# The first MLP's up projection: all 11 column groups as block products of operands without the norm's row factor

## The chip, the cores and the metric

The kernel runs on one core of one Trainium2 chip, as one launch. The metric is the device time of one execution in microseconds. The core's engines are TensorE (PE in the profile, with PEld for its weight loads), VectorE (DVE), ScalarE (ACT), GpSimd (POOL) and SyncE (SP); each works through its own instructions in order and waits on semaphores that the others, or transfers, raise.

## The reference

A trunk of four residual layers over 512 tokens (S) of 1024 features (D), all in float32: attention, MLP, short convolution, MLP. Cut to what matters here:

```python
def conv_ffn(h, norm_g, w_up, conv_w, w_down):
    xn = rms_norm(h, norm_g)                    # h * rsqrt(mean(h*h) + EPS) * norm_g
    u = causal_dwconv(xn @ w_up, conv_w)        # w_up: 1024 x 5632, three taps along the tokens
    g, val = u[..., :D_FF], u[..., D_FF:]       # D_FF = 2816
    return (jax.nn.silu(g) * val) @ w_down      # w_down: 2816 x 1024

h = h + attention_mixer(...);   h = h + conv_ffn(...)   # the MLP of this change
h = h + short_conv_mixer(...);  h = h + conv_ffn(...)
```

The norm multiplies h by two factors: a gain for each feature, and a factor for each token (row), `rsqrt(mean(h*h) + EPS)`. Since the up projection sums over features, the row factor may stand before it or behind it.

## The kernel before

**Precision.** Every float32 operand is split into a high half (ScalarE, `whi`, `p_hi`) and a low half (VectorE, `wlo`, `p_lo`: the operand minus its high half), and each product of blocks is three matmuls: high by high, high by low, low by high.

**Seven products.** Activations lie as features by tokens. A group of an up projection is two column blocks (128 columns each) of the gate and two of the value. Seen as a 2 x 2 block matrix (features 0 to 511 and 512 to 1023; tokens 0 to 255, LEFT, and 256 to 511, RIGHT), its result is made from seven products instead of eight, with sums of blocks ahead of them and sums of results behind them: p1, p7, p3, p6, p2, q5, q4. Each is 24 matmuls of 256 columns (L1078): two column blocks, four blocks of 128 features, three terms. Class `Sevens` plans a group in seven slots (`slot(g, s)`): a slot issues one product, and around it the loads, splits and sums of this group, the group before and the next. The activations' forms of a product (`forms`: p1 is one block, p7 a difference, p6 a sum, and so on) are made once for all groups. The weights' sums that do not depend on the activations are tables in DRAM, "7", "6" and, for the first MLP, "4" (tiles `t`): `table_steps` makes them by DMAs that Pool issues, a plain copy and then an accumulating one, in pairs that build on each other (L114 the accumulating ones, L117 the plain ones).

**The first MLP** has 11 groups. The first two (`PLAIN = 2, 0`) are not made of seven products but of eight plain blocks: `up_seven` runs 192 matmuls of 512 columns (L336 to L338) on `hs_a` and `hs_b`, the halves of h times gain times row factor. While they run, `prepare` makes X_prep, px_prep and Y_prep, again with the row factor, and the forms of the seven products from them; `normed` and `gate_one` do the gates of the plain groups. The norm (class `Norm`) sums squares on ScalarE and VectorE feature block by feature block as the residual adds (L853) of the attention's output projection finish. 12 small matmuls bring the sums together (L410) and spread the row factor over the partitions (L396). The second MLP already works as the change does: all groups are products of h times gain, by `RawForms`, and the results are multiplied by the row factor afterwards (`scaled`).

**The down projection** (`mlp`, second half) makes products of its own in seven phases p1, p7, p2, p6, p3, q5, q4, each over six blocks of the 22 feature blocks (`GROUPS`). Its weights' sums, too, are partly made by accumulating DMAs that Pool issues onto loaded tiles (L289: `p_hi_chain`, `q_lo_chain` and others); ScalarE and VectorE then split them (L315, L316). VectorE joins the results to h (L1609).

**Order.** Most instructions get their place on their engine from a scheduler, which weighs the work by costs. Those in `pin` (`tc.keep_in_program_order`) keep the order of the program among each other; all of Pool's DMAs of the tables and of the weights' sums are pinned. With `strict[0]` on, all of ScalarE's and VectorE's work is pinned too. `norm.finish(at, rows)` puts the small matmuls off by so many microseconds of planned TensorE time.

**Tables.** `FAR` and `BETWEEN` say how many steps of the second MLP's tables are issued after the first MLP's and after its down projection; the others are issued in the short convolution.

Of the kernel before, what the change touches and what calls it, by code (L numbers as in the profile page):

```python
# [57 lines left out]
def trunk(  # L58
# [40 lines left out]
    def table_steps(layer):  # L99

        w = ffn_w_up[layer]
        for n in "76" if layer else "764":
            for g, m in CHUNKS[layer]:
# [3 lines left out]
        for g, m in CHUNKS[layer]:  # L107
            for rows in (slice(0, 256), slice(256, 512)):
                for step in range(4 if layer else 6):
                    n = "764"[step // 2]  # L110
                    to = tables[layer, n, g][rows, 0:m * 256]
                    if step % 2:
                        src = block(*((0, 1), (0, 0), (1, 0))[step // 2], g, m)
                        pin(nc.gpsimd.dma_start(to, src[rows, :], accum_op=ALU.add))  # L114
                    else:
                        src = block(1, 1, g, m) if step == 0 else tables[layer, "76"[step // 2 - 1], g][:, 0:m * 256]
                        pin(nc.gpsimd.dma_start(to, src[rows, :]))  # L117
                    yield

    def table_of(layer, n, group):  # L120
        g, m = next(c for c in CHUNKS[layer] if c[0] <= group < c[0] + c[1])
        return tables[layer, n, g][:, (group - g) * 256:(group - g + 1) * 256].rearrange("(k p) c -> p k c", p=P)

    work_scope = ExitStack()
# [355 lines left out]
    def want_ffn(layer, pairs=NF):  # L480
        for j in range(pairs):
            want(ffn_w_up[layer], 0, 8, j * P, P)
            want(ffn_w_up[layer], 0, 8, DFF + j * P, P)

# [10 lines left out]

    want_ffn(0, 2 * PLAIN[0])

# [8 lines left out]
    def mixed(g):  # L506
        return (ap_.tile([P, 4, S], F32R, tag="o_hi", name=f"o_hi{g}", bufs=2),
                ap_.tile([P, 4, S], F32R, tag=("o_lo", "dl")[g], name=f"o_lo{g}"))
# [445 lines left out]
    dl = ap_.tile([P, 4, S], F32R, tag="dl", name="dl")  # L954
# [13 lines left out]
    sums_far = table_steps(0)  # L968
    next(sums_far)
    fill(PRE)  # L970
    for g in range(len(units) + 2):
        for _ in range(2):
            next(sums_far, None)
# [16 lines left out]

    run(sums_far)
    sums_far = table_steps(1)

    def sum_far(n):
        for _ in range(n):
            next(sums_far, None)

    sum_far(FAR)

    def residual_out(o, acc, nxt):  # L1000
        dve.tensor_tensor(h[:, o, :], acc, h[:, o, :], op=ALU.add)
        nxt.feed(o, h[:, o, :])

    norm = Norm("n1", 0)
    run(output_part((4,), range(2), "c"))
    run(output_part(range(4), (3,), "b"))
    fetch(AHEAD - 1)
    for o in range(4):
        residual(o, last[o])
        norm.halves(o, h[:, o, :])  # L1010
    run(output_part((5,), range(2), "c"))
    run(output_part((6, 7), range(2), "a"))
    fetch(AHEAD)
    for o in range(4, ND):
        run(output_part((o,), (2, 3), "a"))
        residual(o, last[o])
        norm.halves(o, h[:, o, :])
    for o in range(ND):
        norm.squares(o, h[:, o, :])
    norm.finish(LATE)  # L1020
    attn.close()


# [16 lines left out]
    class Blocks:  # L1040
# [3 lines left out]
        def __init__(self, place, layer):  # L1044
            self.layer, self.place, self.parts = layer, place, {}

        def at(self, j, n):
            start = 0 if j < HEAD else HEAD if j < HF else HF
            if start not in self.parts:
                pool_, n_, tag = {0: (self.place, 8, "head"), HEAD: (hsp, HF - HEAD, "hs_b"), HF: (hsp, HF, "hs_a")}[start]  # L1050
# [32 lines left out]
    class Sevens:  # L1083

        def __init__(self, name, mp, groups, block_of):
            self.name, self.mp, self.groups, self.block_of = name, mp, groups, block_of
            self.forms = {n: [mp.tile([P, 4, HT], F32R, tag=f"{n}_{i}", name=f"{n}_{i}{name}") for i in ("hi", "lo")] for n in FORMS}
            self.st, self.wides, self.table, self.fours, self.scaled = {}, {}, None, False, False
# [705 lines left out]
```

## Time and profile before

| | |
|---|---|
| median of 3 runs | 1122.13 us (1121.94 to 1123.9) |
| the profiled execution | 1121.57 us, its span 1119.8 us, clock 1.00 |
| TensorE busy | 1109.3 us, 99% of the span, 7803 matmuls |
| VectorE busy | 958.8 us, 86% |
| ScalarE busy | 680.4 us, 61% |
| Pool busy | 174.3 us, 16% |
| moved by DMA | 220.90 MB |

Times in the rows of the profile are from the start of the span; the prediction is made against the profiled execution and then put to the median. The first MLP's up projection runs from 273.91 us, its down projection to 610.77 us. A row of a group of instructions reads: line, engine, operation, what it writes and reads, how many; then busy microseconds and mean nanoseconds of one, and the idle time of the engine ahead of them with what ended it. A row of the timeline reads: start, duration, engine, line, operation, and in brackets how long the engine had been idle and what released it.

### The profile page before, as it was taken

To read this page: it belongs to the slowest core of one execution; us is meant where nothing else is said; L and a number is where in the kernel's file an instruction comes from. 1 tells how busy PE (TensorE), PEld (TensorE's weight loads), DVE (VectorE), ACT (ScalarE), POOL (GpSimd) and SP (SyncE) were. 2 spreads that over 40 slices of the span, in tenths; PEclk is the share of its full clock that TensorE was granted. 3 is DMA by queue.
4 is the path that set the end of the run, shared out by engine and by line. 5 is a ranking of instruction groups with operands and counts; after the bars stand their busy time and mean duration, and the time that the engine had idled before them with its cause. 6 is when DMAs were issued, how large, how long until landed. Compare 5 with 4: busy or idle time off the path is not lost.

```text
span 1119.8 us, 19731 instructions
## 1 busy us (share of the span) xinstructions
PE 1109.3 (99%) x7803; PEld 1011.9 (90%) x7803; DVE 958.8 (86%) x1482; ACT 680.4 (61%) x1006; POOL 174.3 (16%) x203
## 2 busy tenths in 40 slices
PE   9999999999999999999999999999999999999998
PEld 7888787878899999999999889988999999998886
DVE  6798988987899787888979899767899999999886
ACT  7466676655466667676547355445666656667553
POOL 4011111111111110014401101110112221014300
PEclk9999999999999999999999999999999999999999
DMA  6668777677888787699997955697879877899951
GB/s 195 178 175 199 177 186 196 164 197 196 245 206 199 189 212 192 195 297 198 224 260 195 238 143 141 130 275 178 207 179 218 204 189 189 217 262 205 230 154 57
DMA packets 180012, 220.90 MB, mean 197 GB/s; under 512 B 7788, under 2 KB 143516, under 8 KB 179920
## 3 DMA queue, kind: packets, MB, share of 16 engines
q0 software_dynamic: 48384, 97.43, 43.9%
q1 hardware_dynamic: 131376, 122.14, 34.7%
q8 instruction: 61, 1.00, 0.4%
q14 instruction: 31, 0.25, 0.1%
q10 hardware_dynamic: 160, 0.07, 0.0%
HBM read 214.64 MB, written 53.48 MB: 239 GB/s over the span
## 4 chain that ended last, share of the span: by engine, by line
PE 82%; DVE 7%; DMA 5%; issue 3%; ACT 2%; SPq 0%; ACTq 0%; DVEq 0%; POOLq 0%
PE psb L1078 28%; PE psa L1078 11%; PE psb L1673 10%; PE psa L1673 7%; PE psb L336 4%; PE psb L338 4%; PE psb L337 4%; PE psb L710 2%; PE psa L807 2%; DVE wlo L316 1%; DMA Xc<-in_conv_w_in 1%; DMA raw<-in_conv_w_in 1%; DMA raw<-in_conv_w_out 1%; PE psc L782 1%; PE psa L338 1%
## 5 line engine op out<-in xcount | busy, mean ns | idle before, releaser
L1078 PE MATMUL psb<-p_lo,whi_p 128*128 128x256 f32 x480 | 135.1, 282 | 0.0
L315 ACT ACTIVATE whi<-raw 128x1024 fp32r<-128x1024 f32 (+2 forms) x81 | 83.3, 1029 | 85.3 <-PE psb L337 27.9
L1078 PE MATMUL psb<-p_hi,wlo_p 128*128 128x256 f32 x480 | 135.0, 282 | 0.0
L1078 PE MATMUL psb<-p_hi,whi_p 128*128 128x256 f32 x480 | 134.8, 281 | 0.0
L316 DVE TENSOR_TENSOR wlo<-raw,whi 128x1024 fp32r<-128x1024 f32 (+2 forms) x81 | 95.8, 1183 | 28.0 <-ACT whi L315 27.6
L1078 PEld LDWEIGHTS psb<-p_hi,whi_p 128*128 128x128 f32 x480 | 90.9, 189 | 0.0
L1078 PE MATMUL psb<-q_hi,whi_q 128*128 128x256 f32 x320 | 89.9, 281 | 0.5 <-ACT whi_q L74 0.5
L1078 PEld LDWEIGHTS psb<-p_lo,whi_p 128*128 128x128 f32 x480 | 90.4, 188 | 0.0
L1078 PEld LDWEIGHTS psb<-p_hi,wlo_p 128*128 128x128 f32 x480 | 90.2, 188 | 0.1
L1078 PE MATMUL psa<-p_hi,wlo_p 128*128 128x256 f32 x320 | 90.1, 282 | 0.0
L1078 PE MATMUL psa<-p_lo,whi_p 128*128 128x256 f32 x320 | 90.1, 281 | 0.0
L1078 PE MATMUL psb<-q_lo,whi_q 128*128 128x256 f32 x320 | 90.0, 281 | 0.0
L1078 PE MATMUL psb<-q_hi,wlo_q 128*128 128x256 f32 x320 | 89.9, 281 | 0.0
L1078 PE MATMUL psa<-p_hi,whi_p 128*128 128x256 f32 x320 | 89.8, 281 | 0.0
L336 PE MATMUL psb<-hs_a,whi 128*128 128x512 f32 x192 | 79.3, 413 | 0.0
L338 PE MATMUL psb<-hs_a,wlo 128*128 128x512 f32 x192 | 76.3, 398 | 0.0
L1673 PE MATMUL psb<-act,whi 128*128 128x256 f32 x352 | 63.1, 282 | 0.5 <-DVE act L1031 0.4
L1078 PEld LDWEIGHTS psb<-q_hi,whi_q 128*128 128x128 f32 x320 | 60.6, 189 | 0.8 <-ACT whi_q L74 0.8
L1078 PEld LDWEIGHTS psa<-p_hi,whi_p 128*128 128x128 f32 x320 | 60.6, 190 | 0.1
L1078 PEld LDWEIGHTS psa<-p_lo,whi_p 128*128 128x128 f32 x320 | 60.2, 188 | 0.1
L1078 PEld LDWEIGHTS psb<-q_lo,whi_q 128*128 128x128 f32 x320 | 60.2, 188 | 0.0
L1078 PEld LDWEIGHTS psa<-p_hi,wlo_p 128*128 128x128 f32 x320 | 60.2, 188 | 0.0
(553 smaller groups left out, 3593.6 us busy)
## 6 DMA issues: line engine op xcount, KB each, us to landing
t<-in_ffn_w_up POOLq DMA_DIRECT2D x30, 768.0 KB, 7.8
raw<-in_attn_w_in SPq DMA_DIRECT2D x24, 512.0 KB, 5.4
t<-in_ffn_w_up POOLq DMA_DIRECT2D x12, 1024.0 KB, 10.9
t<-t POOLq DMA_DIRECT2D x14, 768.0 KB, 4.7
X<-in_ffn_w_up SPq DMA_DIRECT2D x20, 512.0 KB, 5.0
Y<-t SPq DMA_DIRECT2D x20, 512.0 KB, 6.7
three<-t SPq DMA_DIRECT2D x20, 512.0 KB, 4.8
W<-in_ffn_w_up SPq DMA_DIRECT2D x20, 512.0 KB, 4.0
```

Of the source, the lines that this page charges most:

```text
L315: return (act.activation(hi[:, at_], raw[:, at_], AF.Copy), dve.tensor_tensor(lo[:, at_], raw[:, at_], f32(hi[:, at_]), op=ALU.subtract))
L316: dve.tensor_tensor(lo[:, at_], raw[:, at_], f32(hi[:, at_]), op=ALU.subtract))
L336: made = [pe.matmul(acc, w[0], rhs[0], start=first, stop=False), pe.matmul(acc, w[0], rhs[1], start=False, stop=False), pe.matmul(acc, w[1 ...
L337: pe.matmul(acc, w[0], rhs[1], start=False, stop=False),
L338: pe.matmul(acc, w[1], rhs[0], start=False, stop=last)]
L710: pe.matmul(ss[e][:, c:c + wide], ql[rows, b * P:n], kl[rows, 0:wide], start=first and b == bs[0], stop=last and b == bs[-1])
L782: pe.transpose(t[:, k * P:(k + 1) * P], w[:, e, k * P:(k + 1) * P], ident)
L807: pe.matmul(out_, w, t[:, first:first + step * (NB - k - 1) + 1:step, :], start=k == 0 and i == 0, stop=k == NB - 1 and i == 1)
L1078: pe.matmul(to, w[a][:, k, c], x[b][:, k, :], start=fresh and i + k + t == 0, stop=i == 1 and k == 3 and t == 2, skip_group_check=not fresh)
L1673: pe.matmul(to, l, r, start=begin and o + t == 0, stop=end and t == 2 and o == (0 if layer else 1), skip_group_check=not fresh)
```

## The change

All 11 groups of the first MLP become seven products; the plain stage with `up_seven`, `prepare`, `normed` and `gate_one` goes. The operands are h times gain, without the row factor: `RawForms.take` writes x_up block by block after each residual add, `make` builds the forms. The squares of the norm are four 1024-wide steps of ScalarE in slot 3 of group 0, their sums four steps of VectorE in slot 4; the small matmuls come later (`LATE` 21 instead of 7), and everything that needs the row factor is held until it is there. The gates of the groups stand in later slots (`tail`). Table "4" is gone: its operand is made by accumulating onto "three". So the first MLP's tables are 24 steps instead of 36, and both MLPs' tables are one sequence: 31 steps (`FAR`) in the attention, 9 (`BETWEEN`) inside the down projection, behind a small Pool instruction `hold` that reads h; before, 8 steps came after the attention and 9 behind the down projection. From the end of the attention's output projection until slot 6 of group 1, ScalarE and VectorE keep program order (`strict`). Two tiles, "four" and "head", are set aside earlier and hold attention tiles until then.

```diff
-NSUMS, NROWS, LATE = 4.0, 3.0, 7.0
+NSUMS, NROWS, LATE = 4.0, 3.0, 21.0
-PLAIN = 2, 0
-FAR, BETWEEN = 8, 9
-CHUNKS = ((2, 3), (5, 3), (8, 3)), ((0, 3), (3, 4), (7, 4))
+FAR, BETWEEN = 31, 9
+CHUNKS = (0, 3), (3, 4), (7, 4)
...
+    sums_far = both_layers()
+    sum_far(1)
     for g in range(len(units) + 2):
-        for _ in range(2):
-            next(sums_far, None)
+        sum_far(min(2, FAR - 1 - 2 * g) if 2 * g < FAR - 1 else 0)
...
         def to_wide(self, g, n, side, acc):
             if self.scaled:
-                dve.tensor_tensor(to, acc, self.row(side), op=ALU.mult)
+                self.norm.scaled(lambda: dve.tensor_tensor(to, acc, self.row(side), op=ALU.mult))
...
-                    if self.fours:
-                        self.load_one(g, "four", self.table("4", g))
+                    c["four"] = c["three" if self.table else "Y"]
+                    if self.scaled and soon:
+                        self.add_block(g, "four", 1, 0)
...
         def tail(p, s):
+            if layer:
+                plan = {0: [(p, 0)], 1: [(p, 1)], 3: [(p, 2)], 4: [(p, 3)], 5: [(p, 4)]}
+            elif p == 0:
+                plan = {4: [(p, 0)], 5: [(p, 1)], 6: [(p, 2), (p, 3)]}
+            else:
+                plan = {0: [(p - 1, 4)], 3: [(p, 0)], 4: [(p, 1)], 5: [(p, 2)], 6: [(p, 3), (p, 4)] if p == HF - 1 else [(p, 3)]}
...
+                if name == "q4" and g == 1 and not layer:
+                    hold = tiny.tile([P, 1], F32, tag="hold", name="hold", bufs=1)
+                    pool.tensor_tensor(hold, h[:, 7, 0:1], h[:, 7, 0:1], op=ALU.add)
+                    sum_far(BETWEEN)
...
         if after_:
             after_.finish()
-            sum_far(BETWEEN)
...
+        strict[0] = True
+        for o in range(4):
+            residual_in_turn(o)
+        raw.make("p1")
+        up.weights_of(0, "p1", "X")
+        raw.make("p7")
+        run(output_part((5,), range(2), "c"))
+        run(output_part((6, 7), range(2), "a"))
+        for o in range(4, ND):
+            run(output_part((o,), (2, 3), "a"))
+            residual_in_turn(o)
+            if o == 4:
+                up.first_sums(0)
+            elif o == 5:
+                raw.make("p6", slice(0, 2))
+        raw.make("p6", slice(2, 4))
+        norm.finish(LATE, LATER)
+        squared = [wides[n] for n in ("ug", "uv", "yg", "yv")]
...
+        norm = mlp(0, mp, blocks, slots_of(up, {
+            (0, 0): lambda: up.weights_of(0, "p6", "three"), (0, 1): lambda: (up.weights_of(0, "p2", "W"), raw.make("p2")),
+            (0, 2): lambda: raw.make("q5"), (0, 3): lambda: (raw.make("q4"), square()), (0, 4): add_squares, (0, 6): lambda: raw.make("p3"),
+            (1, 6): lambda: strict.__setitem__(0, False)}))
```

**Pool's queue in the down projection, before.** `q_hi_chain` and `q_lo_chain` are the weights of phase q4, in the order of its blocks 2 to 5; `t` are tables of the second MLP; `Yc` belongs to the short convolution.

```order
L289 DMA q_hi_chain_0_6196<-in_ffn_w_down 128x2x512
L289 DMA q_lo_chain_0_6230<-in_ffn_w_down 128x512
L289 DMA q_hi_chain_0_6265<-in_ffn_w_down 128x2x512
L289 DMA q_lo_chain_0_6300<-in_ffn_w_down 128x2x512
L117 DMA t_3276<-in_ffn_w_up 256x1024
L114 DMA t_3276<-in_ffn_w_up 256x1024
L117 DMA t_3279<-t_3276 256x1024
L114 DMA t_3279<-in_ffn_w_up 256x1024
```

All four accumulations for q4 stand ahead of the tables; four more steps like these and a ninth follow, then `Yc`. The same place of the changed kernel, where the lines of the two kinds of table steps are L113 and L116:

```order
L289 DMA q_hi_chain_0_6279<-in_ffn_w_down 128x2x512
L289 DMA q_lo_chain_0_6318<-in_ffn_w_down 128x512
L1604 TENSOR_TENSOR hold<-h 128x1
L113 DMA t_1908<-in_ffn_w_up 256x768
L116 DMA t_1906<-in_ffn_w_up 256x1024
L113 DMA t_1906<-in_ffn_w_up 256x1024
L116 DMA t_1909<-t_1906 256x1024
L113 DMA t_1909<-in_ffn_w_up 256x1024
...
L289 DMA q_hi_chain_0_6353<-in_ffn_w_down 128x2x512
L289 DMA q_lo_chain_0_6388<-in_ffn_w_down 128x2x512
```

The accumulations for q4's blocks 4 and 5 have moved from ahead of the tables to behind them (where rows are left out, four more steps like the four above them), and `hold` is new.

**ScalarE at the start of the up projection, before**: splits of the last output weights (`whi<-raw`), halves of the normed h (`hs_a`), squares (`sq_n`):

```order
L372 ACTIVATE hs_a_119<-h,gains 128x512 x3
L381 ACTIVATE sq_n_3391<-h 128x512
...
L315 ACTIVATE whi_3348<-raw_3350 128x1024
L381 ACTIVATE sq_n_3397<-h 128x512
L372 ACTIVATE hs_a_119<-h,gains 128x512 x2
L381 ACTIVATE sq_n_3400<-h 128x512
L315 ACTIVATE whi_3434<-raw_3436 128x1024
```

and in the changed kernel, from the fifth to the last step of group 0 (x_up is h times gain; `three`, `W` and `X` are weights; P7s and Xs are copies of results; `ug`, `uv` and `y_both` receive the squares; `X_3432` belongs to group 1):

```order
L73 ACTIVATE p_hi_3294<-x_up_3302 128x512
L73 ACTIVATE whi_p_3436<-three_3373 128x1024
L73 ACTIVATE psb_3465<-psa_3405 128x512
L73 ACTIVATE whi_p_3467<-W_3430 128x1024
...
L73 ACTIVATE q_hi_3300<-x_up_3302 128x1024
L73 ACTIVATE ug_3282<-h 128x1024
L73 ACTIVATE uv_3283<-h 128x1024
L73 ACTIVATE y_both_3281<-h 128x1024 x2
L73 ACTIVATE Xs_3537<-psb_3465 128x512
L73 ACTIVATE whi_q_3539<-three_3373 128x1024
L73 ACTIVATE whi_p_3573<-X_3432 128x1024
```

The halves of the normed h are gone from this place, the forms and the weights of group 0 have come to it, and the squares, now four wide steps, stand ahead of the weights of q4. VectorE holds the low halves in the same order, and the sums of the squares ahead of the low half of group 1's first weights:

```order
L73 TENSOR_TENSOR wlo_q_3540<-three_3373,whi_q_3539 128x1024
L73 TENSOR_TENSOR ug_3282<-ug_3282,uv_3283 128x1024
L73 TENSOR_TENSOR ug_3282<-ug_3282,y_both_3281 128x1024 x2
L73 TENSOR_TENSOR nacc_n_3280<-ug_3282 128x512
L73 TENSOR_TENSOR wlo_p_3574<-X_3432,whi_p_3573 128x1024
```

These sums were seven short steps of the scheduler's placing (`nacc_n<-nacc_n,sq_n`, 128x512) before; now they are four, at a fixed place.

More of the change, by code (lines that the diff above doesn't have):

```diff
@@ L967, in trunk, with both_layers, sum_far @@
     waiting = {}
-    sums_far = table_steps(0)
-    next(sums_far)
+    def both_layers():
+        for layer in range(2):
+            yield from table_steps(layer)
+    sums_far = both_layers()
+    def sum_far(n):
+        for _ in range(n):
+            next(sums_far, None)
+    sum_far(1)
     fill(PRE)
     for g in range(len(units) + 2):
-        for _ in range(2):
-            next(sums_far, None)
+        sum_far(min(2, FAR - 1 - 2 * g) if 2 * g < FAR - 1 else 0)
         if g < len(units):
@@ L989, in trunk @@
     fill(1e9)
[L991 to L1020, printed above, removed]
     attn.close()
@@ L1510, in conv_seven, with mlp @@
         return ys, place
[L1512 to L1513 removed]
+    def mlp(layer, mp, blocks, slots):
         acts, c1, c2 = {}, {}, {}
@@ L1759, in trunk @@
         late = slice(3, 4)
-        more = {0: lambda: up.weights_of(0, "p6", "three"), 1: lambda: (up.weights_of(0, "p2", "W"), raw.make("p2", late)),
-                2: lambda: (raw.make("q5", late), raw.make("q4", late)), 5: lambda: raw.make("p3"), 6: lambda: strict.__setitem__(0, False)}
-        def slot(g, s):
-            up.slot(g, s)
-            if g == 0 and s in more:
-                more[s]()
-        mlp(1, norm, mp, (blocks, [(lambda g=g, s=s: slot(g, s)) for g in range(HF + 1) for s in range(7)]))
+        mlp(1, mp, blocks, slots_of(up, {
+            (0, 0): lambda: up.weights_of(0, "p6", "three"), (0, 1): lambda: (up.weights_of(0, "p2", "W"), raw.make("p2", late)),
+            (0, 2): lambda: (raw.make("q5", late), raw.make("q4", late)), (0, 5): lambda: raw.make("p3"),
+            (0, 6): lambda: strict.__setitem__(0, False)}))
 _INS = [
```

188 lines of the change are left out of this document (76 added, 112 removed).

## The prediction

> **What bounds the kernel now.** I read the page's busy times and its chain of waits first, then the busy table by stretch of time, then the two stages that the change touches. The page says:
>
> ```profile
> PE 1109.3 (99%) x7803; PEld 1011.9 (90%) x7803; DVE 958.8 (86%) x1482; ACT 680.4 (61%) x1006; POOL 174.3 (16%) x203
> PE 82%; DVE 7%; DMA 5%; issue 3%; ACT 2%; SPq 0%; ACTq 0%; DVEq 0%; POOLq 0%
> ```
>
> TensorE works 1109.3 of 1119.8 us: matmuls removed shorten the kernel by their own time, and every wait put in front of TensorE lengthens it, since almost none is there to absorb it. By stretch (columns: PE, PEld, DVE, ACT, POOL busy, clock, DMA share, GB/s):
>
> ```profile
> 273.90:319.90 46.00, 46.00 (x206) 37.45 (x205) 41.75 (x71) 25.24 (x35) 4.84 (x7) 1.00 0.81 215
> 359.90:379.80 19.90, 19.90 (x170) 19.90 (x170) 16.17 (x23) 13.24 (x17) 3.03 (x3) 1.00 0.83 209
> 560.00:580.00 20.00, 18.97 (x158) 18.57 (x157) 14.85 (x20) 10.18 (x15) 0.91 (x1) 1.00 0.96 257
> 580.00:600.00 20.00, 19.59 (x165) 19.39 (x165) 17.59 (x24) 10.89 (x17) 2.01 (x3) 1.00 0.93 253
> ```
>
> The first is the plain stage that the change removes: TensorE has no gap, and VectorE is busy 41.75 of 46.00. The second is one group of seven products. The last two, in the down projection, hold the only idle TensorE time near the change: 1.03 + 0.41 us.
>
> **Term 1, the products saved.** The last matmul before the plain stage, its first and the first after it, and three starts of one psa product, one group apart:
>
> ```profile
> 273.67 0.40 PE L338 MATMUL psa<-o_hi,wlo 128*128 128x512 f32 x1
> 273.91 0.39 PE L336 MATMUL psb<-hs_a,whi 128*128 128x512 f32 x1
> 319.89 0.28 PE L1078 MATMUL psa<-p_hi,whi_p 128*128 128x256 f32 x1
> ...
> 337.17 2.85 PE psa L1078 x24
> 357.07 2.82 PE psa L1078 x24
> 376.93 2.84 PE psa L1078 x24
> ```
>
> The plain stage is 319.89 − 273.91 = 45.98 us. It holds 12 small matmuls of the norm, which only move; they cost about 0.9 us, the surplus of the 45.98 over 192 matmuls at the 0.235 us between two starts (273.67 to 273.91). A group of seven is 19.9 us (357.07 − 337.17, 376.93 − 357.07). Two groups replace 45.1 us by 39.8: **−5.3 us**, if the operands are there in time.
>
> **Term 2, group 0's operands.** Before, the plain stage needed only halves of the normed h, and the product operands were built under its 46 us. Now they must be built between the last residuals and TensorE's first product. Prices, from the stretch 262 to 320:
>
> ```profile
> L316 DVE TENSOR_TENSOR wlo<-raw,whi 128x1024 fp32r<-128x1024 f32 x8 | 9.8, 1223 | 0.7 <-ACT whi L315 0.5
> L315 ACT ACTIVATE whi<-raw 128x1024 fp32r<-128x1024 f32 x8 | 8.5, 1062 | 6.3 <-PE psb L337 4.5 <-PE psa L337 1.4 <-ACT sq_n L381 0.2
> L372 ACT ACTIVATE hs_a<-h,gains 128x512 fp32r<-128x512 f32 x8 | 5.4, 715 | 5.0 <-DVE h L853 5.0
> L1027 ACT ACTIVATE p_hi<-Y_prep 128x512 fp32r<-128x512 f32 x6 | 3.8, 630 | 4.7 <-DVE Y_prep L1331 4.7
> 262.22 2.09 DVE L853 TENSOR_TENSOR h<-psb,h 128x512 f32<-128x512 f32 x3 [2.21 <-PE psb L338]
> ```
>
> So a 1024-wide step is 1.22 us on VectorE and 1.06 on ScalarE; a 512-wide one 0.70 (2.09 / 3) and 0.63, or 0.72 with the gain. From 262.2 to the weights of group 1's p1, VectorE has 13 short steps and 17 long ones, 29.8 us; ScalarE has 8 with gain, 5 short and 16 long, 25.9 us. Had each engine never waited, VectorE would be through at 292.0; were it all one chain, at 317.9. That chain is mostly real: a high half is made on ScalarE, its low half on VectorE, the next sum on VectorE, its high half on ScalarE, both engines in a pinned order. I walked it by these prices. Residuals and gains 0 to 3 are done at 265.7; p1's low half and weights at 269.2; p7's sum and halves at 272.7; residual 4, its gain, p7's weights at 276.3; residuals 5 to 7 with p6's two half-width operands at 283.1; p6's weights and the negated copy of p1's result that p6 adds onto near 284.7. TensorE wants p6 at 273.9 + 2 × 2.84 = 279.6, so it is 5 us behind there. ScalarE's q4 operand ends near 292.5; the four squares (4 × 1.06) hold back the weights of q4 to about 298.4; VectorE's adds (3 × 1.22 + 0.70 = 4.4) stand ahead of the low half of group 1's p1 weights, ready near 304.2. That product ends near 306.9; without a gap the seventh product would end at 273.9 + 7 × 2.84 = 293.8: 13 us lost. Then the gate of group 0, the row factors and the normal steps of group 1 share a VectorE that already has 16.17 of 19.90 us in a normal group: 0 to 6 us more. I take **+15**; the bounds are 8 (the squares and adds, 8.6 us, found half in gaps) and 20 (all of the above).
>
> **Term 3, the Pool queue in the down projection.** This is the large one. In program order the changed Pool queue has first `hold`, which waits for VectorE's second join of the q5 phase; then 9 table steps; and only then the accumulations that complete the weights of q4's blocks 4 and 5. Before, those accumulations stood ahead of the tables. What the table steps take is in the timeline of Pool:
>
> ```profile
> 556.95 1.20 POOL L289 DMA_DIRECT2D q_lo_chain<-in_ffn_w_down  x1 [1.63 <-DVE wlo L316]
> 557.68 1.09 POOL L117 DMA_DIRECT2D t<-in_ffn_w_up  x1
> 572.46 0.91 POOL L114 DMA_DIRECT2D t<-in_ffn_w_up  x1 [13.69 <-DMA t<-in_ffn_w_up]
> 582.15 0.57 POOL L117 DMA_DIRECT2D t<-t  x1 [8.79 <-DMA t<-in_ffn_w_up]
> 589.94 0.87 POOL L114 DMA_DIRECT2D t<-in_ffn_w_up  x1 [7.21 <-DMA t<-t]
> 590.50 0.87 POOL L117 DMA_DIRECT2D t<-in_ffn_w_up  x1
> 604.27 0.88 POOL L114 DMA_DIRECT2D t<-in_ffn_w_up  x1 [12.90 <-DMA t<-in_ffn_w_up]
> 613.04 0.58 POOL L117 DMA_DIRECT2D t<-t  x1 [7.89 <-DMA t<-in_ffn_w_up]
> 620.31 0.87 POOL L114 DMA_DIRECT2D t<-in_ffn_w_up  x1 [6.70 <-DMA t<-t]
> 581.96 0.68 DVE L1609 TENSOR_TENSOR h<-h,psa 128x512 f32<-128x512 f32 x1
> ```
>
> Each accumulation or copy waits on Pool itself until the transfer before it has landed: six waits, 62.6 us from the first of these eight steps to the last. The eight of the changed queue are the same kinds at the same 1 MB, behind one that waits for nothing. The last row is the join: on the old clock Pool is released at 582.6. TensorE reaches q4's block 4 at about 604.06, 54 matmuls of 0.12 us before the next stage begins at 610.77:
>
> ```profile
> 604.06 0.40 PE L1673 MATMUL psb<-act,whi 128*128 128x256 f32 x2
> 610.77 0.39 PE L336 MATMUL psb<-hs_a,whi 128*128 128x512 f32 x1
> ...
> q_hi_chain<-in_ffn_w_down POOLq DMA_DIRECT2D x2, 512.0 KB, 10.7
> X<-in_ffn_w_up POOLq DMA_DIRECT2D x1, 512.0 KB, 5.8
> ```
>
> The cover is 604.06 − 582.6 = 21.5 us. The last two rows are issue to landing of such transfers. TensorE runs in order, and no other product stands before block 4, so what exceeds the cover is a stall. For the eight steps I bound: above, 62.6 us; below, the smaller steps of 768 KB with little beside them,
>
> ```profile
> 40.20 0.59 POOL L117 DMA_DIRECT2D t<-in_ffn_w_up  x1
> 45.46 0.99 POOL L114 DMA_DIRECT2D t<-in_ffn_w_up  x1 [4.67 <-DMA t<-in_ffn_w_up]
> 53.90 0.58 POOL L117 DMA_DIRECT2D t<-t  x1 [7.45 <-DMA t<-in_ffn_w_up]
> 59.11 1.05 POOL L114 DMA_DIRECT2D t<-in_ffn_w_up  x1 [4.62 <-DMA t<-t]
> ```
>
> 18.9 us for half the steps, taken unscaled 2 × 18.9 + 8 = 46. I take 56: the first links run beside the weight loads as before, the later ones beside less, because the stall stops those loads. In front come the hold and one step, 2 us; behind, 1.2 us to issue, 9 us to land (between 5.8 and 10.7), 2.3 us to split the weights (1.06 + 1.22). 56 + 2 + 1.2 + 9 + 2.3 − 21.5 = **+49**, with 36 and 57 as bounds. Behind the same accumulations stand the loads for the short convolution; they come later, and the work after them too, but TensorE is then already late by the stall, so I add nothing.
>
> **Terms near nothing.** The tables no longer run beside the loads of the down weights at 557 to 583, so the 1.4 us of gaps may go: **−1.4**, bounds −2 and 0. Eight steps instead of seven remain for the short convolution, and Pool's first accumulation for the second MLP has slack there:
>
> ```profile
> 782.61 1.34 POOL L1105 DMA_DIRECT2D X<-in_ffn_w_up  x1 [12.35 <-DVE wlo_p L1029]
> ```
>
> One more step is 7 to 13 us by the rows above: 0 to 1 us. "Four" by accumulation instead of a table read, for 11 groups, is what the second MLP already does at 19.9 us a group: 0.
>
> All granted clocks above are 1.00, and no row here has TensorE idle for long. The Trainium skill ("TensorE: Matmul & The Clock Gate", Part 1, the HAM clock gate) says that idle time lets the clock fall to half and that some 4 us of work bring it back; by it a stall this long would add an estimated 2 us, and no trace here can show it.
>
> **Sum.** −5.3 + 15 + 49 − 1.4 = +57.3 on the profiled run's 1121.57 us: 1178.9; the median of the runs is 0.56 above that. I say **1179 us**.
>
> **Rivals.** (B) Group 0 keeps up: ScalarE and VectorE overlap better than my walk and lose 2 us. For it: both have idle time together; against it: the pinned order. Then −5.3 + 2 + 49 − 1.4 = +44: 1166. (C) Pool comes back in time: only group 0's loss counts, −5.3 + 15 = +10: 1132. It decides from eight steps in about 7 us (21.5 − 2 − 1.2 − 9 − 2.3), or a hold released 49 us sooner; the six waits above are against it. (D) Neither loss: the saving alone, −5.3 − 1.4: 1115, faster than before. It needs C's condition and group 0 on time. (E) Quick links: six waits near 4.7 us, the shortest above, with 8 us of issue, are 36 us; the stall is then 29 us, and with +15 − 6.7 the time is 1159.
>
> The Trainium skill ("DMA: Bandwidth & Descriptors", Anatomy of one DMA, SWDGE path) fits 2.0 us plus bytes / 436 GB/s, 4.4 us for 1 MB, and speaks for E; the waits of 6.70 to 13.69 us speak against it.
>
> **How the numbers follow.** Likeliest A (both losses as summed) 0.75; B 0.11; E 0.07; C 0.04; D 0.03. A's own range, by its bounds (8 + 36 to 20 + 57, less 6.7), is 1159 to 1192. For 8 in 10 I reach to 1155 and 1196, which takes in B and E. A measurement of this kernel tells about 0.2% (2.2 us) from no change. Faster has D, 0.03, and a hundredth for what I don't see; within 0.2%, 0.01; slower the rest, 0.95.
>
> **What would show it.** Right: TensorE idle some 50 us before the second third of q4, its releaser the split of q_hi_chain and, before that, Pool's accumulation, with the six waits in Pool's timeline ahead of it; gaps of 10 to 20 us in the first 40 us of the first up projection, released by ScalarE and VectorE; groups after that at 19.9 us. Wrong: a Pool queue whose accumulations for q4 are issued before the tables land, or group 0's products back to back from 273.9.

## The result, and the profile after

The changed kernel takes 1169.14 us (median of four runs, 1166.88 to 1169.96), the kernel before 1122.04 us beside it: a ratio of 1.0415, 95% interval 1.0394 to 1.0435. It is slower by 47.1 us; the forecast was 57 slower, 1179 us with 1155 to 1196 around it.

The page of the changed kernel, the engines' busy time, the chain's shares and the granted clock in 40 slices:

```profile
PE 1096.0 (94%) x7947; PEld 1003.0 (86%) x7947; DVE 976.6 (84%) x1497; ACT 674.5 (58%) x988; POOL 181.5 (16%) x204
PE 57%; issue 15%; DVE 13%; DMA 9%; ACT 4%; POOL 1%; DVEq 0%; POOLq 0%; ACTq 0%
PEclk9999999999889999999996699999999999999999
```

TensorE is no longer busy all the time, and its clock, which was 9 in every slice before, falls in two places. By stage, first the kernel before, then the changed one (up projection, down projection, the rest; columns as in the prediction):

```profile
273.90:496.05 222.15, 222.15 (x1694) 213.59 (x1692) 190.69 (x258) 144.78 (x191) 25.88 (x24) 1.00 0.79 212
496.05:610.77 114.72, 113.23 (x951) 112.42 (x950) 99.86 (x135) 69.43 (x98) 28.62 (x28) 1.00 0.97 228
610.77:1119.80 509.03, 503.76 (x3424) 463.14 (x3422) 441.82 (x572) 291.88 (x377) 78.95 (x70) 1.00 0.78 190
```

```profile
273.90:510.93 237.03, 219.46 (x1838) 216.22 (x1837) 210.71 (x273) 144.39 (x180) 35.79 (x29) 0.97 0.74 179
510.93:666.71 155.78, 111.84 (x951) 110.89 (x949) 104.05 (x142) 69.34 (x98) 31.43 (x32) 0.86 0.83 193
666.71:1167.80 501.09, 494.05 (x3424) 452.37 (x3422) 438.98 (x571) 289.24 (x376) 77.06 (x68) 1.00 0.77 187
```

The up projection is 14.9 us longer, the down projection 41.1, and the rest, whose code the change hardly touches, 7.9 us shorter. That last number was in no term of the sum. TensorE's longest waits in the changed kernel:

```profile
PE psb L1592 <- ACT act L1000: 42.1, 1, 42.1
PE psb L1051 <- ACT Xs L73: 5.5, 1, 5.5
```

The view names ScalarE's last step ahead of the wait. What stands behind it is in Pool's timeline of the changed kernel, and in ScalarE's and TensorE's:

```profile
565.67 0.88 POOL L289 DMA_DIRECT2D q_lo_chain<-in_ffn_w_down  x1 [0.61 <-DVE wlo L316]
593.45 0.57 POOL L1604 TENSOR_TENSOR hold<-h 128x1 f32<-128x1 f32 x1 [26.90 <-DVE h L1528]
593.98 0.90 POOL L113 DMA_DIRECT2D t<-in_ffn_w_up  x1
594.59 0.87 POOL L116 DMA_DIRECT2D t<-in_ffn_w_up  x1
604.61 0.87 POOL L113 DMA_DIRECT2D t<-in_ffn_w_up  x1 [9.15 <-DMA t<-in_ffn_w_up]
613.69 0.57 POOL L116 DMA_DIRECT2D t<-t  x1 [8.21 <-DMA t<-in_ffn_w_up]
...
643.97 0.87 POOL L113 DMA_DIRECT2D t<-in_ffn_w_up  x1 [4.96 <-DMA t<-t]
644.98 1.24 POOL L289 DMA_DIRECT2D q_hi_chain<-in_ffn_w_down  x1
655.65 1.06 ACT L315 ACTIVATE whi<-q_hi_chain 128x1024 fp32r<-128x1024 f32 x1 [43.14 <-DMA q_hi_chain<-in_ffn_w_down]
657.28 0.80 PE L1592 MATMUL psb<-act,whi 128*128 128x256 f32 x2 [42.14 <-ACT act L1000]
```

`hold` is released at 593.45, TensorE's last matmul ahead of block 4 starts at 614.87, and the accumulation that block 4 needs is issued at 644.98, behind the last of the nine table steps, and landed at 655.6. The wait is Pool's queue, as forecast.

### The profile page after: what moved, and what is told of

Its sections match the earlier page's. It is cut to its first block, busy times and chain, and to the rows that moved or that the text cites. A ratio compares the mean times of both kernels' runs of the same rounds, so it can differ in the third digit from the quotient of the medians.

```text
span 1167.8 us, 20018 instructions
## 1 busy us (share of the span) xinstructions
PE 1096.0 (94%) x7947; PEld 1003.0 (86%) x7947; DVE 976.6 (84%) x1497; ACT 674.5 (58%) x988; POOL 181.5 (16%) x204
## 4 chain that ended last, share of the span: by engine, by line
PE 57%; issue 15%; DVE 13%; DMA 9%; ACT 4%; POOL 1%; DVEq 0%; POOLq 0%; ACTq 0%
PE psb L1051 11%; PE psb L1592 9%; PE psa L1592 7%; DMA three<-in_ffn_w_up 5%; PE psb L336 4%; PE psb L338 4%; PE psb L337 4%; PE psa L1051 4%; DVE wlo_p L1002 3%; PE psb L705 2%; DMA t<-in_ffn_w_up 2%; PE psa L802 2%; PE psa L338 1%; DVE wlo L316 1%; PE psa L337 1%
## 5 line engine op out<-in xcount | busy, mean ns | idle before, releaser
L1051 PE MATMUL psb<-p_hi,whi_p 128*128 128x256 f32 x528 | 147.6, 280 | 4.1 <-ACT whi_p L1000 1.9
L1051 PE MATMUL psb<-p_hi,wlo_p 128*128 128x256 f32 x528 | 147.4, 280 | 2.6 <-DVE wlo_p L73 2.6
L1051 PE MATMUL psb<-p_lo,whi_p 128*128 128x256 f32 x528 | 147.2, 279 | 0.0
L1051 PE MATMUL psb<-q_hi,whi_q 128*128 128x256 f32 x352 | 99.5, 283 | 8.1 <-ACT Xs L73 5.5
L1592 PE MATMUL psb<-act,whi 128*128 128x256 f32 x352 | 63.7, 285 | 43.3 <-ACT act L1000 42.1
L1051 PEld LDWEIGHTS psb<-p_hi,wlo_p 128*128 128x128 f32 x528 | 100.2, 190 | 3.3 <-DVE wlo_p L73 3.2
L316 DVE TENSOR_TENSOR wlo<-raw,whi 128x1024 fp32r<-128x1024 f32 (+2 forms) x73 | 85.9, 1177 | 20.4 <-ACT whi L315 20.2
L1051 PE MATMUL psb<-q_hi,wlo_q 128*128 128x256 f32 x352 | 99.5, 283 | 2.0 <-DVE wlo_q L1002 1.9
L1051 PEld LDWEIGHTS psb<-p_lo,whi_p 128*128 128x128 f32 x528 | 100.3, 190 | 0.0
L1592 PEld LDWEIGHTS psb<-act,whi 128*128 128x128 f32 x352 | 55.7, 196 | 44.0 <-ACT act L1000 42.3
L1051 PEld LDWEIGHTS psb<-q_hi,wlo_q 128*128 128x128 f32 x352 | 67.3, 191 | 3.4 <-DVE wlo_q L1002 3.1
```

The source lines that it names most:

```text
L316: dve.tensor_tensor(lo[:, at_], raw[:, at_], f32(hi[:, at_]), op=ALU.subtract))
L1051: pe.matmul(to, w[a][:, k, c], x[b][:, k, :], start=fresh and i + k + t == 0, stop=i == 1 and k == 3 and t == 2, skip_group_check=not fresh)
L1592: pe.matmul(to, l, r, start=begin and o + t == 0, stop=end and t == 2 and o == (0 if layer else 1), skip_group_check=not fresh)
```

## The experiments

**The tables behind the accumulations.** In the changed kernel, `hold` and its steps go from inside q4 to the end of the down projection:

```diff
-                if name == "q4" and g == 1 and not layer:
-                    hold = ...; pool.tensor_tensor(hold, ...); sum_far(BETWEEN)
...
         if after_:
             after_.finish()
+            hold = ...; pool.tensor_tensor(hold, ...); sum_far(BETWEEN)
```

> The changed kernel with the Pool instruction hold and its nine table steps moved behind the end of the down projection, so that all accumulations for q4 stand ahead of them again; everything else as in the change. Theory (the queue): the gap of 42.3 us in q4 goes, and with it the matmuls at the lower clock behind it (29 of about 0.21 instead of 0.11 us, 2.9 us): 1169 - 45 = 1124 us, between 1120 and 1128. Rival (the tables themselves, or their traffic, are too long for any place here): the short convolution's first accumulation, now behind them, comes late instead, and TensorE waits there for 20 us or more: 1140 or above.

Measured: 1144.27 us, 1.0182 of before (1.0163 to 1.0200). The gap in q4 is gone, but the kernel is only 25 us faster than the changed one, where 45 was expected. The changed place also puts off what `hold` waits for. Pool's timeline and TensorE's longest wait of this run:

```profile
613.26 0.57 POOL L1624 TENSOR_TENSOR hold<-h 128x1 f32<-128x1 f32 x1 [41.36 <-DVE h L1528]
...
669.00 1.67 POOL L1082 DMA_DIRECT2D Yc<-in_conv_w_in  x1
PE psb L1051 <- ACT whi_p7c L1000: 8.4, 1, 8.4
```

Pool starts the tables at 613.26 and comes to the convolution's first accumulation, `Yc`, at 669.00; before, it did so at 621.44. TensorE waits 8.4 us there, where the rival had said 20 or more. So the theory was right about q4, and the rival about the place of the new wait and the time: the same queue made a wait behind it. Whether `hold` or the steps make it, this run can't tell; the run after the next has the steps in the same place without `hold`, and is 12.4 us faster.

**No hold, tables left in place.** The line with `pool.tensor_tensor(hold, ...)` is taken out; an unread tile keeps its 32 bytes.

> The changed kernel without the instruction hold (its 32 bytes are kept by an unread tile), the nine table steps left where they are, ahead of the accumulations for q4's blocks 4 and 5. Theory (the six waits on transfers make the stall, hold only puts their start off): Pool begins the steps when it is done with the accumulation before, near 566.6 us on the clock of the changed kernel instead of 593.5; they take 51 to 63 us, and issue, landing and split 13: the weights come at 631 to 642 for a need at 615, so TensorE waits 16 to 27 us instead of 42: 1142 to 1154 us. Rival (hold alone makes the stall): 1124 us.

Measured: 1152.75 us (two runs), 1.0257 of before (1.0229 to 1.0284), inside the theory's range. Pool and TensorE:

```profile
566.59 1.10 POOL L113 DMA_DIRECT2D t<-in_ffn_w_up  x1
567.18 1.08 POOL L116 DMA_DIRECT2D t<-in_ffn_w_up  x1
...
627.50 1.23 POOL L289 DMA_DIRECT2D q_hi_chain<-in_ffn_w_down  x1
640.17 0.58 PE L1592 MATMUL psb<-act,whi 128*128 128x256 f32 x1 [20.28 <-ACT act L1000]
```

The steps begin 27 us sooner and take longer (59.3 us from 567.18 to 626.49, the start of the last, against 49.4 from 594.59 to 643.97). The stall falls from 42.1 to 20.3 us. So the late start adds 21.8 us to it, and the steps make 20.3 even without `hold`; what `hold` would cost without the steps, no run shows.

**No hold, tables behind.** The first two together.

```diff
-                    hold = ...; pool.tensor_tensor(hold, ...); sum_far(BETWEEN)
...
         if after_:
             after_.finish()
+            sum_far(BETWEEN)
```

> The changed kernel with the nine table steps behind q4's accumulations, as in the run with the tables behind, but without the instruction hold (an unread tile keeps its 32 bytes), so that Pool begins them at some 572 us and not at 613. Theory (the queue): neither q4 nor the short convolution waits for Pool; against the changed kernel the 42.3 us go and the slow matmuls behind them: 1122 to 1128 us. Rival: the tables beside the loads of the down weights make waits of 5 us and more there: 1130 us or above.

Measured: 1131.88 us, 1.0076 of before (1.0053 to 1.0100): 37 us faster than the changed kernel, and no long wait is left in q4 or the convolution. It is 4 us above the range expected, in the rival's; but the waits of 5 us beside the down weights, by which the rival got there, are not in the trace. TensorE's longest waits are now in group 0 of the up projection and, with 2.4 us, in the down projection. In the profiled execution (1134.66 us) the down projection is 39.1 us shorter than in the changed kernel and the rest 5.0 longer, in several short waits.

```profile
PE psb L1051 <- ACT Xs L73: 5.5, 1, 5.5
PE psa L1592 <- ACT act L1000: 2.4, 1, 2.4
```

**An address, twice.** The 7.9 us that the rest gained lie in the 256-column matmuls. By the starts in the traces, these were 118.3 ns apart before and are 113.3 ns apart in the changed kernel, in the same code, from the up projection to the end. `hold` is a tile of 4 bytes in a partition; it takes 32, and every pool behind it is shifted by 32. The weights' halves are in a pool ahead of it, the forms, the moving operand of the products, in pools behind it. I read the addresses in the compiled programs, which the traces don't hold: the halves of the weights 32 behind a multiple of 64 bytes in both kernels, the forms at a multiple of 64 before and 32 behind one after. First the kernel before with an unread tile of that size:

```diff
-    far = ctx.enter_context(...)
+    far = ctx.enter_context(...); pool.memset(tiny.tile([P, 1], F32, tag="pad", name="pad", bufs=1), 0.0)
```

> The kernel before with one more tile of 4 bytes in a partition in the pool tiny, which takes 32 bytes and shifts the address of every pool behind it by 32; it is written once by Pool and read by nothing. In the profile of the changed kernel the 256-column matmuls of the MLPs and the convolution start every 113.3 ns, before every 118.3 ns; hold takes such a tile. Theory (addresses): the moving operands of the products lie at a multiple of 64 bytes before, 32 behind one in the changed kernel, as the weights do in both; with the shift the 118.3 become 113.3, 25 us over some 5000 matmuls: 1097 us, between 1093 and 1101. Rival (rhythm): TensorE falls into the quicker rhythm by its first waits at 274 us, whatever the addresses: no change, 1122 us.

and then the same line in the changed kernel, which makes its shift 64:

> The changed kernel with one more such tile, so that the pools behind are shifted by 64 bytes against before and the moving operands lie at a multiple of 64 bytes again. Theory (addresses): 5292 matmuls at 118.3 instead of 113.3 ns, 26 us more: 1195 us, between 1190 and 1199, and the stall in q4 of the same length within 3 us. Rival (rhythm, or code): 1169 us.

Measured: before with the shift 1115.78 us (nine runs, 1111.09 to 1126.10), 0.9932 of before (0.9901 to 0.9963); the changed kernel with 64 bytes 1183.95 us, 1.0536 (1.0520 to 1.0553). The rhythm follows the shift in both: 113.3 ns in the first and 119.5 in the mean in the second. One psa product of 24 matmuls (one of the kind that the prediction's rows have at 2.84 us), in the kernel before with the shift, then in the changed kernel with 64 bytes, where this one is slower than the mean:

```profile
366.73 2.72 PE psa L1078 x24
```

```profile
363.95 2.91 PE psa L1051 x24
```

The times follow it only in part: −8 us for 25 expected, +15 for 26. In the second, the slower matmuls cover waits that stood open: TensorE's idle time in the up projection falls from 17.6 us (237.03 − 219.46) to 12.6:

```profile
273.50:513.13 239.63, 226.99 (x1838) 225.24 (x1838) 214.48 (x276) 146.95 (x180) 35.79 (x29) 0.97 0.75 179
```

In the first, TensorE runs ahead of the loads. The profiled execution took 1125.98 us, 10 more than the median of the nine, so its waits are likely longer than those of a middle one, of which there is no trace. ScalarE and VectorE in it at the start of the convolution, and TensorE's wait:

```profile
623.96 1.06 ACT L315 ACTIVATE whi<-raw 128x1024 fp32r<-128x1024 f32 x1 [10.07 <-DMA raw<-in_conv_w_in]
617.14 0.16 DVE L432 TENSOR_TENSOR rb_n<-ra_n,rh_n 128x4 f32<-128x4 f32 x1
625.04 1.23 DVE L316 TENSOR_TENSOR wlo<-raw,whi 128x1024 fp32r<-128x1024 f32 x1 [7.74 <-ACT whi L315]
626.18 0.16 DVE L434 SCALAR_TENSOR_TENSOR ncol_n<-rb_n,ry_n 128x4 f32<-128x4 f32 x1
PE psc L396 <- DVE ncol_n L434: 7.6, 1, 7.6
```

The last step of the norm, 0.16 us long, stands on VectorE behind the split of a weight whose load landed only at 623.96.

**Which address.** Two more shifts of the kernel before: 32 bytes in the first pool, which moves weights and forms, and that with another 32 in `tiny` (a line as in the first shift), which moves the forms again.

```diff
-    const = ctx.enter_context(...)
+    const = ctx.enter_context(...); pool.memset(const.tile([P, 1], F32, tag="pad", name="pad"), 0.0)
```

> The kernel before with 32 bytes more in the first pool, so that the weights' halves and the products' moving operands are both shifted by 32: weights at a multiple of 64 bytes, moving operands 32 behind one. Theory (the two must stand alike to a multiple of 64): they differ by 32 as before, so the 256-column matmuls start every 118.3 ns as before, 1122 us. Rival (the moving operands alone count): every 113.3 ns, and a time like that of the run with the moving operands shifted, 1111 to 1126 us.

> The kernel before with 32 bytes more in the first pool and 32 more in the pool tiny: the weights' halves and the products' moving operands both lie at a multiple of 64 bytes. Theory (the two must stand alike to a multiple of 64): the 256-column matmuls start every 113.3 ns, the time is 1111 to 1126 us as with the first shift. Rival (both must lie 32 behind a multiple): 118.3 ns, 1122 to 1128 us.

Measured, one run each: 1128.43 and 1118.14 us. The psa products of the first and of the second:

```profile
370.62 2.84 PE psa L1078 x24
```

```profile
366.03 2.72 PE psa L1078 x24
```

With the bytes by which weights and forms lie behind a multiple of 64, the place before the shifts being that of the compiled program: 32 and 0 give 118.3 ns, 32 and 32 give 113.3, 0 and 32 give 118.3, 0 and 0 give 113.3. So neither address alone counts, but the distance of the two, and by the compiled program they agree where it is quick. Why they should is not shown.

**The up projection alone.** The run without hold and with the tables behind, without any tile in hold's place, so that the forms lie as in the kernel before.

> The changed kernel without hold, with the nine table steps behind q4's accumulations, and without any tile in the place of hold: the moving operands lie at a multiple of 64 bytes as in the kernel before, so that what is left of the change is the up projection and the shorter tables. Theory from the traces (the up projection is 17.8 us longer in the run with 64 bytes of shift than before, since group 0 waits more and at a lower clock than I worked out): 1122 + 18 = 1140 us, between 1136 and 1144. Rival, the prediction's own terms 1 and 2 (-5.3 + 15): 1132 us, between 1126 and 1135.

Measured: 1140.08 us (1139.95 to 1140.26), 1.0124 of before (1.0070 to 1.0178). It is the theory's number, and 8 above the rival's. Its up projection, and two stretches in it:

```profile
273.90:512.44 238.54, 224.67 (x1838) 222.81 (x1837) 214.02 (x276) 146.80 (x180) 35.78 (x29) 0.97 0.74 179
273.90:300.00 26.10, 16.50 (x114) 15.34 (x114) 16.70 (x18) 17.39 (x22) 1.30 (x1) 0.91 0.26 50
320.00:340.00 20.00, 15.73 (x107) 15.04 (x107) 19.26 (x26) 11.07 (x15) 3.81 (x3) 0.83 0.58 143
```

At the old rhythm and with the queue mended, the up projection is 16.4 us longer than the plain stage and nine groups (238.54 − 222.15). TensorE is idle for 13.9 us, 9.6 in the first stretch and 4.3 in the second, and its clock is down in both.

**The squares later.** On the mended kernel (no hold, tables behind, hold's bytes kept):

```diff
-... (0, 3): lambda: (raw.make("q4"), square()), (0, 4): add_squares, ...
+... (0, 3): lambda: raw.make("q4"), (0, 5): lambda: (square(), add_squares()), ...
```

> The run before this one, and beside it the four squares and their sums moved from slots 3 and 4 of group 0 to slot 5, behind the copy of Xs, the weights of q4 and the weights of group 1's p1. Theory (the squares hold back Xs): the gap of 5.4 us ahead of q5 goes and with it some 27 matmuls at 0.213 instead of 0.113 us, 2.7 us: 8 us faster than without it, between 5 and 9. Rival (the row factor is then late, or VectorE has no room anywhere): within 2 us.

Measured: 1128.84 us, 1.0048 (1.0029 to 1.0066), 3.0 us below the run without it instead of 8, with executions that overlap. The wait on Xs fell from 5.5 us to

```profile
PE psb L1051 <- ACT Xs L73: 1.7, 1, 1.7
```

so the squares did hold back Xs. But most slow matmuls remained: by the starts in the trace, the excess of those 0.16 to 0.30 us apart in the up projection is 6.2 us where it was 8.1. The other waits of the first groups are left, and so are the slow matmuls behind them.

**A shorter stretch in program order.** That, and `strict` off at slot 6 of group 0 instead of group 1.

> The run before this one, and beside it program order for ScalarE and VectorE kept only until slot 6 of group 0 instead of group 1. Theory (pinned gates): the gaps of 5 us at 325 to 335 us come from group 0's row factors and gates standing in program order ahead of group 2's weights on VectorE; the scheduler puts the weights first, the gaps and the slow matmuls behind them (3 us) go: 5 to 8 us faster. Rival: VectorE has too much to do there in any order: within 2 us.

Measured: 1139.85 us, 1.0133 (1.0088 to 1.0177), 11 us slower, where I expected 5 to 8 faster. In the profiled run 3.8 us of it lie ahead of the up projection, in the first 100 us, where the granted clock was 0.97 and the code is the same; the rest is mostly in the up projection, where VectorE's low halves of q weights now come late seven times instead of six and for 3.5 us instead of 1.8:

```profile
PE psb L1051 <- DVE wlo_q L1002: 3.5, 7, 0.8
```

The pinned order was not the reason for the gaps at 325 to 335. From 325 to 333 VectorE is busy for 7.89 of 8.00 us with it and for 7.80 without, which speaks for the rival's reason, too much work in any order; that is not shown, and what would help was not found.

**Only the tables.** The kernel before with its plain stage and the shift of 32 bytes, and of the change only the shorter tables, all but seven steps of them issued in the attention and none in the down projection:

```diff
-FAR, BETWEEN = 8, 9
+FAR, BETWEEN = 41, 0
...
-        for n in "76" if layer else "764":
+        for n in "76":
...
-                for step in range(4 if layer else 6):
+                for step in range(4):
...
+    sums_far = both_layers()
...
-        up.fours, up.scaled = layer == 0, not base
+        up.fours, up.scaled = False, not base
...
-                        if self.scaled and soon:
+                        if self.table and soon:
```

> The kernel before (with its plain stage), the moving operands shifted by 32 bytes, and of the change only the tables: no table 4, its operand accumulated onto three, and 41 of the 48 steps in the attention, none in the down projection, seven in the short convolution as before. Theory (with the quicker matmuls, transfers bound the down projection and the start of the convolution, and the tables are the part of them that can go elsewhere): the waits of the first shifted run there, up to 8 us at 618 us, go: 1105 to 1112 us, the best so far. Rival (they moved into a stretch that is as full, or the loads are late by themselves): 1113 to 1118 us.

Measured: 1106.90 us (1104.57 to 1111.07), 0.9837 of before (0.9798 to 0.9875): faster than both kernels, and 9 us faster than the shift alone. No wait of TensorE is longer than

```profile
PE psb L1078 <- ACT Xsc L1139: 1.4, 1, 1.4
```

And the same without the shift:

> The last run's kernel (the plain stage, and of the change only the tables) without the shift of 32 bytes, so with 256-column matmuls every 118.3 ns. Theory (the tables' traffic costs something only where TensorE runs ahead of the loads): the kernel before has 1.4 us of gaps in the stretch that the tables leave, so the time is 1120 to 1123.5 us, and of the 17 us between the last run and before all but 2 need the shift. Rival (the shorter tables pay by themselves): 1118 us or less.

Measured: 1120.39 us, 0.9964 (0.9948 to 0.9980), 3.2 us below the kernel before beside it (1123.60), inside the theory's range. 13.5 of the nearly 17 us need the shift. The tables by themselves pay 3.2 us, and 8.9 with the shift: most of their worth is in waits that only a quicker TensorE meets.

## Why the prediction was right, and where not

The time, its side and the mechanism of the largest term were right. That the size came out within 10 us is luck in part: a term too small by 7 us and a gain of 15 that no term had went against each other.

**Term 1, the products saved (−5.3).** A group at 118.3 ns a start is 19.9 us in the changed code too, and none of the runs speaks against the saving. The 0.235 us between two starts of the plain stage are 0.233 by the trace, which takes 0.4 us from it. It did not count that the rhythm itself could change: in the changed kernel a later group takes 19.0 us, not the 19.9 named as a sign.

**Term 2, group 0's operands (+15, bounds 8 and 20): too small, also in its upper bound.** The walk was good where it gave times. It had p6 ready near 284.7; the matmuls of p6 start at 284.7. It had the weights of q4 at 298.4 and those of group 1's p1 at 304.2; they are split at 298.6 and 304.1. That product ends at 307.9 for 306.9. But neither of these two weights held TensorE up: it has no gap ahead of q4 or of that product, since the wait on Xs and the slow matmuls behind it had already made it as late. That the end agrees is luck in part. Three things were missing. First, the wait on Xs: the walk let the squares hold back q4's weights, but not the copy of Xs, which q5 needs and which stands behind the same squares. ScalarE of the changed kernel, and TensorE:

```profile
293.95 1.99 ACT L73 ACTIVATE y_both<-h 128x1024 f32<-128x1024 f32 x2
295.85 0.57 ACT L73 ACTIVATE Xs<-psb 128x512 f32<-128x512 f32 x1
296.47 0.58 PE L1051 MATMUL psb<-q_hi,whi_q 128*128 128x256 f32 x1 [5.49 <-ACT Xs L73]
```

That moved the wait within group 0; its end stayed near where the walk had it. Second, groups 1 and 2: I gave them 2 us of the 0 to 6, and TensorE is idle for 3.3 us from 325 to 333 alone, with another wait and the slow stretch behind it. By the starts in the run of the up projection alone, the first seven products end 14 us late, for the 13 of the walk, and the next fourteen take 48.7 us where 39.8 and the 0.9 of the small matmuls were due: 8 us for my 2. Third, the clock. After the waits, matmuls ran at half of it (windows of the changed kernel, the last behind the stall in q4):

```profile
296.50:303.00 6.50, 6.50 (x31) 6.50 (x32) 5.50 (x6) 2.87 (x3) 0.00 (x0) 0.52 0.48 154
325.00:333.00 8.00, 4.73 (x38) 4.28 (x36) 7.75 (x12) 6.92 (x8) 1.29 (x1) 1.00 0.90 221
333.00:340.00 7.00, 5.46 (x26) 5.26 (x26) 6.57 (x8) 1.47 (x3) 2.52 (x2) 0.53 0.45 105
657.30:664.50 7.20, 6.66 (x29) 6.36 (x30) 6.50 (x9) 5.08 (x7) 0.00 (x0) 0.50 0.16 42
```

6.5 us at 0.52 are 3.1 us lost, 5.46 at 0.53 2.6, 6.66 at 0.50 3.3. In the up projection that is 5.7 us, part of the 14 and the 8. The measured change of the up projection at the old rhythm, queue mended, is +16.4 (the run of it alone) where the two terms gave 9.7: term 2 is some 22 us.

**Term 3, Pool's queue (+49, bounds 36 and 57): right, a little large.** The cover was worked out as 21.5 us and is 21.4 (593.45 to 614.87). The eight steps took 49.4 us for the 56 taken, and the landing 10.7 for 9. The stall is 42.3 us by the matmuls' starts, 45.6 with the slow matmuls behind it. I had said that the later links would be quicker, because the stall stops the weight loads. They were hardly so: the first three waits are 9.15, 8.21 and 5.03 us, the second three, of the same kinds and inside the stall, 9.55, 7.29 and 4.96. What is shorter is all six against before (13.69, 8.79, 7.21 and 12.90, 7.89, 6.70), the first three no less than the others; why is not shown. The rows of Pool's timeline for the three that are not shown above:

```profile
619.29 0.86 POOL L113 DMA_DIRECT2D t<-in_ffn_w_up  x1 [5.03 <-DMA t<-t]
630.27 0.88 POOL L113 DMA_DIRECT2D t<-in_ffn_w_up  x1 [9.55 <-DMA t<-in_ffn_w_up]
638.44 0.57 POOL L116 DMA_DIRECT2D t<-t  x1 [7.29 <-DMA t<-in_ffn_w_up]
```

**The term of −1.4** was right about its cause and nearly nothing here. With no table in the down projection (the last run above) the stage has 0.07 us of idle TensorE for the 1.49 before:

```profile
497.50:610.64 113.14, 113.07 (x950) 112.69 (x949) 100.08 (x135) 69.72 (x98) 25.36 (x23) 1.00 0.78 181
566.00:594.00 28.00, 28.00 (x250) 28.00 (x249) 25.86 (x36) 16.63 (x24) 1.10 (x3) 1.00 0.68 171
594.00:604.00 10.00, 9.35 (x83) 9.16 (x82) 7.58 (x9) 5.85 (x8) 1.46 (x3) 1.00 0.88 227
```

The last two rows are of the changed kernel: no idle time while `hold` keeps the tables back, and 0.65 us as soon as they run. With 0.61 us from 510.93 to 566, that is 1.26 us ahead of the stall.

**What stands in place of the rest: −15 us.** With forms and weights apart by 32 bytes, the address taken away and nothing else, the changed kernel is 1183.95 us, 60.1 above the kernel beside it (1123.86); the sum had said 57.3. That is the kernel that I had priced. The shift by `hold`'s 32 bytes gave 14.8 us back; with the two executions profiled, 2.6 of them are in the up projection, 3.5 in the down projection and 9.0 behind it.

**The rivals.** B (group 0 keeps up), C and D (Pool in time) fell: both losses were there in the trace. E (quick links) named the direction of the miss in term 3, but its 36 us for eight steps were 49.4. The Trainium skill's fit for one transfer ("DMA: Bandwidth & Descriptors", Anatomy of one DMA, SWDGE path), by which 1 MB would take 4.4 us, is less than half of what the table loads of 1 MB took: Pool waited 9.15 us for the first of them in the stall, and 13.69 us before.

## What to carry to other kernels

Before a transfer is put ahead of others on a queue, count what stands behind it, and for which cover: six waits on 1 MB each, begun late behind `hold`, cost 42 us because one accumulation stood behind them. When TensorE is the bound, a wait can cost more than its length: behind the one of 5.5 us, matmuls at half clock lost 3.1 more. And look at the start of every operand by its address: 32 bytes that nobody reads gave 8 us to the kernel before, more than the 5.3 that the change saves in matmuls.

## What the runs showed of the hardware

**Addresses.** 256-column float32r matmuls that load new weights each time started every 113.3 ns or every 118.3 (119.5 in the mean in one run), and a shift of one operand by 32 bytes against the other changed one into the other, in all four combinations and in three stages of the program. By the addresses of the compiled programs, they are quick where both operands lie at the same offset to a multiple of 64 bytes. The 512-column ones of the plain stage (233 ns) say nothing on this: both their operands are in pools ahead of `tiny`, and no run shifted one against the other. The Trainium skill ("TensorE: Matmul & The Clock Gate", Part 2, the step-by-step section) has the two operands on independent read ports, so that loading weights does not take bandwidth from a running matmul; the 5 ns, which hang on both addresses together, raise a doubt whether the two are quite independent, but no run here shows where they arise.

**The clock.** Behind a wait of 5.5 us TensorE ran at half clock for 6 us, behind one of 42 us for 7. The clock also fell at 333.4, after waits of 1.4 and 1.9 us and in a third of 1.5, with matmuls between, and stayed down for 6.8 us; in the run without hold and with the tables behind, it fell after a wait of 2.4 us and one of 1.0, and came back after 3.4 us:

```profile
588.25:591.60 3.35, 3.35 (x18) 3.35 (x18) 1.65 (x2) 2.74 (x4) 0.88 (x1) 0.50 0.70 219
```

The Trainium skill (same page, Part 1, the HAM clock gate) gives an idle window of some 3.4 us for the fall and about as long for the return: that the clock halves agrees; the return took as long in the row above, and nearly twice as long behind the long waits; and the fall came at these two places without any single wait of that length. The estimate of 2 us behind the stall, in the prediction, was 3.3.
